# Input projection and mixers' preparation: the elementwise steps of GpSimd put on VectorE

## The chip, the cores and the metric

One core of a Trainium2 chip runs the whole kernel. The metric is the time of one execution on the device in microseconds (us). Five engines work side by side, each through its own queue in order: TensorE (PE: matmuls; PEld: its weight loads), VectorE (DVE), ScalarE (ACT), GpSimd (POOL) and SyncE (SP), which here only issues DMAs. Engines wait for each other by semaphores.

## The reference, cut to what matters

One layer of a hybrid encoder for 656 tokens (16 meta, 512 prompt, 8 x 16 sample), model width 1024:

```
x += 0.5 * SwiGLU_1(RMSNorm(x))
h  = RMSNorm(x);  c = h @ w_in
y  = concat[MLA(c_A), RG-LRU(c_B), GatedDeltaNet(c_C), RWKV7(c_D)] @ w_out;  x += y
x += 0.5 * SwiGLU_2(RMSNorm(x))
final RMSNorm
```

The change lies in the line `c = h @ w_in` and in what prepares the four mixers from its columns: the attention's queries and keys get a rotation (rope) and a normalization, the others a short convolution or a shift by one token, decays, and normalized keys. All of it is float32.

## The kernel before

A float32 product is made of three fast ones: each operand is split into a high part (rounded to the fast format) and a low part (operand minus high part), and high x high, high x low and low x high are summed in PSUM. The split of a weight is one ACT instruction (`whi`, the high part) and one subtraction (`wlo`, the low part).

The execution has four stages: the first SwiGLU (0 to 466 us), the input projection with the mixers' preparation (466 to 793 us), the mixers' tiles with attention over the cache and the output projection (793 to about 1015 us), and the second SwiGLU. The projection has 24 chunks of 128 columns (`project`, L2116). A chunk loads 512 KB of weights on SP's queue, splits them (`wload`, L406: raw, `whi` and `wlo` have two buffers each), and issues 48 matmuls into two of three PSUM buffers (`mm`); DVE then evacuates the two results, multiplied by the row scale `R`. The first chunk (`scale` given) has its `wlo` on DVE, the other 23 on POOL (L2118).

Between the chunks run the preparations as tasks. `Tasks` (L202) is a planner: a modelled clock (`Clock`, L118) charges every instruction, 1.04 ns an element + 70 for DVE, 1.9 ns + 130 for POOL, and the task of the lowest rank that is ready in the model is written next; the compiler's scheduler then orders each engine's queue by that program order and by what its own model has ready. The projection has the last rank (5) and fills what the others leave. POOL's steps before the change are these:

- `rsqrt` (L345): with `pool` true, two DVE instructions and then ten on POOL; with `pool` false, nine on DVE.
- `rope_rows` (L1640): two products on DVE (out of PSUM), their sum on POOL; for `kpe` and for each of four query heads, in two column halves. ACT then squares the head (`s`) and PE sums the squares (`pick`).
- `shifted` (L1157) and `conv` (L1398): a memset and three small copies before and after which ACT starts the mix (`cv`); `rwkv_decay` (L1208) and `rwkv_keys` (L1231): one difference `Wp` and the products with the last decay of each block (`kh`, `bh`); `lru` (L1591): one product; `mla_in` (L1665): one copy of `kpe` into each key head `kh`; `lora_weights` (L1184): the low part of two small weights.
- In the third stage `gdn_front` (L1508): one product `D` a tile; `rwkv_out`, `gdn_out`: the `rsqrt` of tiles 1 and 5; `mla_sample`: an `rsqrt` of 128 columns.

POOL also makes the triangular inverses (`invert`, L852), the products with the sample masks (`sample_tile`) and some copies for the sample's attention.

Of the kernel before, what the change touches and what calls it, by code (L numbers as in the profile page):

```python
# [228 lines left out]
class Kern:  # L229
# [114 lines left out]

    def rsqrt(self, v, n, pool=True):  # L345

        nc = self.nc
        V = nc.vector
        def tmp(nm):
            if n > 32:  # L350
                return self.t(self.mp, [128, 128], "PN" if nm == "rsr" else "Pn", bufs=2)[:v.shape[0], :n]
            return self.t(self.sp, [128, 32], nm, bufs=2)[:v.shape[0], :n]

        y, q = tmp("rsy"), tmp("rsq")
        V.tensor_scalar(y.bitcast(I32), v.bitcast(I32), 1, None, op0=OP.logical_shift_right)
        V.tensor_scalar(y.bitcast(I32), y.bitcast(I32), -1.0, float(0x5f3759df), op0=OP.mult, op1=OP.add)
        if pool:
            r = tmp("rsr")
            G = nc.gpsimd
            G.tensor_tensor(q, y, y, OP.mult)  # L360
            G.tensor_tensor(q, q, v, OP.mult)
            G.tensor_scalar(q, q, -0.5, 1.5, op0=OP.mult, op1=OP.add)
            G.tensor_tensor(y, y, q, OP.mult)
            G.tensor_tensor(q, y, y, OP.mult)
            G.tensor_tensor(q, q, v, OP.mult)
            G.tensor_scalar(r, q, 0.375, -1.25, op0=OP.mult, op1=OP.add)
            G.tensor_tensor(q, q, r, OP.mult)
            G.tensor_scalar(q, q, 1.875, None, op0=OP.add)
            G.tensor_tensor(v, q, y, OP.mult)
            return  # L370

        V.tensor_tensor(q, y, y, OP.mult)
        V.scalar_tensor_tensor(q, q, -0.1875, v, op0=OP.mult, op1=OP.mult)
        V.scalar_tensor_tensor(y, q, 0.5625, y, op0=OP.add, op1=OP.mult)
        V.tensor_tensor(q, y, y, OP.mult)
        V.scalar_tensor_tensor(q, q, 64.0 / 9, v, op0=OP.mult, op1=OP.mult)
        V.scalar_tensor_tensor(q, q, -10.0 / 3, q, op0=OP.add, op1=OP.mult)
        V.scalar_tensor_tensor(v, q, 5.0, y, op0=OP.add, op1=OP.mult)
# [26 lines left out]

    def wload(self, src, kk, dma, eng=None):  # L406
        nc = self.nc
        raw = self.t(self.wp, [128, self.wk, 128], "wraw")
        hi = self.t(self.wp, [128, self.wk, 128], "whi", F32R)
        lo = self.t(self.wp, [128, self.wk, 128], "wlo", F32R)  # L410
        raw, hi, lo = raw[:, :kk], hi[:, :kk], lo[:, :kk]
        dma.dma_start(raw, src)
        nc.scalar.activation(hi, raw, AF.Copy)
        (eng or nc.vector).tensor_tensor(lo, raw, hi.bitcast(F32), OP.subtract)
        return [(hi[:, k], lo[:, k]) for k in range(kk)]
# [32 lines left out]

    def norm_rows(self, acc, blks, pool, inverse=False):

        ps = self.t(self.pp, [128, 512], "mx")[:, :6].rearrange("p (b o) -> p b o", o=1)
        for b in blks:
            c, n = BLK[b]
            self.nc.tensor.matmul(ps[:n, b, :], acc[:, c:c + n], self.one[:, 0:1], start=True, stop=True)
        r = self.compact(ps, 1, blks, 1.0 / 1024, EPS, "nrow")
        ri = self.t(self.sp, [128, 6, 1], "nrowi", bufs=1) if inverse else None
        if inverse:
            self.nc.vector.tensor_copy(ri[:, blks[0]:blks[-1] + 1], r[:, blks[0]:blks[-1] + 1])
        self.rsqrt(r[:, blks[0]:blks[-1] + 1, 0], len(blks), pool)
        if inverse:  # L460
            q = ri[:, blks[0]:blks[-1] + 1]
            self.nc.vector.tensor_tensor(q, q, r[:, blks[0]:blks[-1] + 1], OP.mult)
            return r, ri
        return r
# [9 lines left out]

    def row_scale(self, acc, blks, cols, pool, inverse=False):


        r = self.norm_rows(acc, blks, pool, inverse)
        yield
# [587 lines left out]

    def rows(self, ps, blks, mul, add, tag, pool=True):

# [3 lines left out]
        for i, (_, n, _) in enumerate(blks):  # L1073
            if n < 128:
                V.memset(c[:, i], 1.0)
            V.tensor_scalar(c[:n, i], ps[:n, i], mul, add, op0=OP.mult, op1=OP.add)
        self.rsqrt(c.rearrange("p b c -> p (b c)"), 4 * nb, pool)
        return c
# [58 lines left out]
    def unit(self, sq, mul, dst, l, op):  # L1137
# [5 lines left out]
        r = self.compact(ps, 2, list(range(6)), mul, EPS * mul, "c2")  # L1143
        self.rsqrt(r.rearrange("p b c -> p (b c)"), 12, False)
        e = self.t(self.rp, [128, 6, 2, 64], "exp6", bufs=1)
# [11 lines left out]
    def shifted(self, j, R, sh, tails, x):  # L1157

        nc = self.nc
        V, S, G = nc.vector, nc.scalar, nc.gpsimd  # L1160
        rv = R[:, 529:].rearrange("p (b c) -> p b c", b=8)
        G.memset(R[:, 0:1], 0.0)
        G.tensor_copy(rv[:, :, 0], sh[:, j])
        G.tensor_copy(tails[:, j, 0:1], R[:, 528:529])
        G.tensor_copy(tails[:, j, 1:], rv[:, :, 16])
        t = self.t(self.rp, [128, LC], "cv", bufs=2)
# [17 lines left out]
    def lora_weights(self, src):  # L1184
# [8 lines left out]
        for i in range(2):  # L1193
            r = slice(64 * i, 64 * i + 64)
            nc.gpsimd.tensor_tensor(lo[r], raw[r, i], hi[r, i].bitcast(F32), OP.subtract)
        return hi, lo
# [11 lines left out]
    def rwkv_decay(self, x, wab, rm, dec):  # L1208
# [9 lines left out]
        for hp in range(2):  # L1218
            V.tensor_scalar(Wp[:, hp], Wp[:, hp], 1.0, None, op0=OP.add)
            V.tensor_tensor_scan(Wi[:, hp], rm, Wp[:, hp], 0.0, op0=OP.mult, op1=OP.add)  # L1220
            nc.gpsimd.tensor_tensor(Wp[:, hp], Wi[:, hp], Wp[:, hp], OP.subtract)
            S.activation(W[:, hp], Wi[:, hp], AF.Exp, scale=C1)
# [8 lines left out]
    def rwkv_keys(self, hp, xk, dw, put):  # L1231

        nc = self.nc
        V, S, G = nc.vector, nc.scalar, nc.gpsimd
        W, Wi, Wp, ta = (t[:, hp] for t in dw)
# [22 lines left out]
        for src, n in ((ki, "kh"), (bt, "bh")):  # L1258
            d = rt()
            for a, t, e in ((0, 16, 16), (16, 64, 528), (528, 16, NT)):  # L1260
                v = lambda z: z[:, a:e].rearrange("p (c t) -> p c t", t=t)
                G.tensor_tensor(v(d), v(src), v(W)[:, :, t - 1:t].to_broadcast([128, (e - a) // t, t]), OP.mult)
            put(n, hp, d)
# [112 lines left out]
    def rwkv_out(self, cx, oT, y):  # L1376
# [10 lines left out]
        yield  # L1387
        es = self.spread(self.rows(self.sums(sq, bl), bl, 1.0 / 64, GN_EPS, "c4", cx["b"] not in (2, 3, 4)), bl)
        yield
# [8 lines left out]
    def conv(self, c, buf, j, tails, w, bias=None):  # L1398

        V, G = self.nc.vector, self.nc.gpsimd  # L1400
        cv = c[:, 531:].rearrange("p (b t) -> p b t", b=8)
        G.memset(c[:, 0:3], 0.0)
        G.tensor_copy(cv[:, :, 0:3], buf[:, j])
        G.tensor_copy(tails[:, j, 0], c[:, 528:531])
        G.tensor_copy(tails[:, j, 1:], cv[:, :, 16:19])
        y = self.t(self.rp, [128, LC], "cv", bufs=2)
# [101 lines left out]
    def gdn_front(self, ti, X, scr, gt, ctxs):  # L1508
# [14 lines left out]
        for c0, T, b in blks:  # L1523
# [12 lines left out]
            S.activation(D, D, AF.Exp)  # L1536
            G.tensor_tensor(D, D, be[:T, b].unsqueeze(2).to_broadcast([T, 4, T]), OP.mult)
            yield
# [31 lines left out]
    def gdn_out(self, cx, oT, y):  # L1570
# [5 lines left out]
        yield  # L1576
        es = self.spread(self.rows(self.sums(sq, bl), bl, 1.0 / 64, EPS, "c4", cx["b"] not in (2, 3, 4)), bl)
        yield
# [12 lines left out]
    def lru(self, j, xc, gb, w, h0, hl):  # L1591
# [21 lines left out]
        V.scalar_tensor_tensor(b, a, 1.0, b, op0=OP.add, op1=OP.mult)  # L1613
        nc.gpsimd.tensor_tensor(b, b, ti, OP.mult)

# [24 lines left out]
    def rope_rows(self, dst, ps, c0, n):  # L1640
# [4 lines left out]
        V.tensor_tensor(a[64:96, :n], ps[96:128, :n], self.rope[96:128, c0:c0 + n], OP.mult)  # L1645
        self.nc.gpsimd.tensor_tensor(dst[64:96, c0:c0 + n], dst[64:96, c0:c0 + n], a[64:96, :n], OP.add)

# [17 lines left out]
    def mla_in(self, cq, ckv, sm, w, outs):  # L1665
# [38 lines left out]
        for h in range(4):  # L1704
# [13 lines left out]
            for c0, n in ((0, 400), (400, 128)):  # L1718
                ps = self.t(self.pp, [128, 512], "mx")
                T_.matmul(ps[:64, :n], wuk[:, h], cn[:, c0:c0 + n], start=True, stop=True)  # L1720
                S.activation(k[:64, c0:c0 + n], ps[:64, :n], AF.Copy)
            G.tensor_copy(k[64:96], kpe[64:96, :528])
            s = self.t(self.mp, [128, NT], "s3", bufs=1)
# [13 lines left out]
        V.tensor_scalar(qr, qr, 1.0 / 96, EPS, op0=OP.mult, op1=OP.add)  # L1737
        self.rsqrt(qr.rearrange("p b c -> p (b c)"), 24, False)
        V.tensor_tensor(qr, qr, rr[:, 0].unsqueeze(2).to_broadcast([128, 6, 4]), OP.mult)
# [95 lines left out]
    def mla_sample(self, new, w, caches, y):  # L1835
# [63 lines left out]
        self.rsqrt(ss[:, :128], 128)  # L1899
        self.rsqrt(ss[:, 128:], 4, False)  # L1900
        yield
# [101 lines left out]
def build(tc, A, O):  # L2003
    with ExitStack() as ctx:
# [18 lines left out]
        with ExitStack() as f:  # L2023
# [38 lines left out]
            def scale():  # L2062
                yield from K.row_scale(acc0, allb, cols, False, True)
                K.acc = K.t(K.hp_, [128, NT], "acc")
# [25 lines left out]
        with ExitStack() as f:  # L2090
# [25 lines left out]
            def project(c, ev, scale=None):  # L2116
                with tc.high_priority() if scale else ExitStack():
                    w = K.wload(A["w_in"][c], 8, nc.sync, None if scale else G)  # L2118
                ps = [K.t(K.pp, [128, 512], "mm", bufs=3) for _ in range(2)]
# [73 lines left out]
            def gate_chunks():  # L2193
                s_ = K.row_scale(K.acc, allb, cols, False)
                yield from plain(7, sm, s_)
# [301 lines left out]
        with ExitStack() as f:  # L2497
# [13 lines left out]
            def last(h):  # L2511
                r = K.norm_rows(K.acc, [b for b in fb if (b > 3) == h], False)
                yield
# [10 lines left out]

            K.ffn(x, fcols, lambda: K.row_scale(acc, fb, fcols, False, True), F, "norm_ffn2", norm=last, rows=False)
        pctx.close()
# [118 lines left out]
```

## Time and profile before

| | us |
|---|---|
| median of three runs | 1526.97 (1524.2 to 1529.06) |
| the profiled execution | 1526.97 |
| its span | 1525.0 |
| PE, DVE, ACT, POOL busy | 1448.5, 1094.0, 610.1, 195.4 |
| mean granted TensorE clock | 0.969 |

The span is what the trace covers; some 2 us lie around it. A busy PE is not PE at its peak, since the ends of matmuls are modelled, so that what it waits for is read from its waits. The granted clock has two levels here: 1.00 is 2.4 GHz and 0.50 is 1.2 GHz; a value between them for a stretch is a mixture.

### The profile page before, as it was taken

What the parts mean: (1) busy time and instruction counts of PE and PEld (TensorE: products, weight loads), DVE (VectorE), ACT (ScalarE), POOL (GpSimd) and SP (SyncE); (2) the same over time, 40 slices, a digit from 0 to 9 for tenths busy, and PEclk for the clock granted to TensorE, in tenths of its full rate; (3) what the DMA queues carried; (4) which work ended last, traced back from release to release, by engine and by line L of the source; (5) the groups of instructions that cost most, each with busy time, mean ns of one, the idle gap of its engine ahead of it and who ended that gap; (6) DMA issues with size and microseconds to landing.
All of it is one profiled execution on the core that took longest, in us unless ns stands there. A gap on an engine that the chain in (4) does not pass through costs nothing.

```text
span 1525.0 us, 26202 instructions
## 1 busy us (share of the span) xinstructions
PE 1448.5 (95%) x10158; PEld 1349.1 (88%) x10158; DVE 1094.0 (72%) x2408; ACT 610.1 (40%) x1162; POOL 195.4 (13%) x392
## 2 busy tenths in 40 slices
PE   7999999999999989999987999999999999999996
PEld 6899999999998757878776877689999999999996
DVE  7987858686885367664765555685996966878787
ACT  6534525252442253354423323232652533434351
POOL 0000000000003333122532523510000000000000
PEclk9999999999999999999888989999999999999997
DMA  8131222223224201212267443384122222222221
GB/s 274 46 107 56 81 75 69 95 70 98 70 85 151 64 32 37 86 55 97 100 208 192 114 111 93 93 242 151 56 80 73 90 91 84 87 81 84 81 58 69
DMA packets 106636, 148.14 MB, mean 97 GB/s; under 512 B 20160, under 2 KB 68304, under 8 KB 106512
## 3 DMA queue, kind: packets, MB, share of 16 engines
q1 hardware_dynamic: 103376, 143.99, 30.1%
q10 hardware_dynamic: 3136, 2.47, 0.6%
q8 instruction: 80, 1.31, 0.4%
q14 instruction: 44, 0.36, 0.1%
HBM read 119.88 MB, written 26.56 MB: 96 GB/s over the span
## 4 chain that ended last, share of the span: by engine, by line
PE 79%; DVE 9%; issue 3%; POOL 3%; ACT 3%; DMA 2%; SPq 0%; ACTq 0%; DVEq 0%; POOLq 0%
PE mx L189 63%; PE mm L189 17%; DVE x L189 2%; DVE rsq L189 1%; DVE n L189 1%; POOL qh L189 1%; DVE P L189 1%; POOL kx L189 1%; DMA r<-in_w_out 0%; DVE acc L189 0%; POOL rsq L189 0%; DMA lrow<-q 0%; DVE rx L189 0%; DVE row L189 0%; DMA scr_rw<-kx 0%
## 5 line engine op out<-in xcount | busy, mean ns | idle before, releaser
L189 ACT ACTIVATE whi<-wraw 128x512 fp32r<-128x512 f32 (+2 forms) x260 | 168.0, 649 | 262.2 <-PE mx L189 164.4
L189 PE MATMUL mx<-f,whi 128*128 128x256 f32 (+4 forms) x1200 | 258.9, 309 | 0.0
L189 PE MATMUL mm<-n,whi 128*128 128x400 f32 (+2 forms) x1024 | 213.1, 327 | 11.7 <-ACT n L189 6.4
L189 PEld LDWEIGHTS mx<-f,whi 128*128 128x128 f32 x1200 | 192.5, 189 | 0.5 <-ACT f L189 0.2
L189 PE MATMUL mx<-n,whi 128*128 128x320 f32 (+1 forms) x1088 | 188.3, 312 | 2.7 <-ACT n L189 2.4
L189 DVE TENSOR_TENSOR wlo<-wraw,whi 128x512 fp32r<-128x512 f32 (+2 forms) x233 | 155.8, 670 | 40.5 <-ACT whi L189 38.1
L189 PEld LDWEIGHTS mm<-n,whi 128*128 128x128 f32 x1024 | 164.4, 195 | 21.5 <-ACT n L189 6.4
L189 PEld LDWEIGHTS mx<-n,whi 128*128 128x128 f32 x1088 | 167.7, 189 | 3.8 <-ACT n L189 2.8
L189 ACT ACTIVATE whi<-wsum 128x512 fp32r<-128x512 f32 x160 | 100.5, 631 | 176.1 <-PE mx L189 140.6
L189 PE MATMUL mx<-e,whi 128*128 128x320 f32 (+1 forms) x904 | 159.3, 312 | 0.0
L189 PE MATMUL mx<-f,wlo 128*128 128x384 f32 (+4 forms) x600 | 150.8, 309 | 0.0
L189 PEld LDWEIGHTS mx<-e,whi 128*128 128x128 f32 x904 | 140.8, 189 | 0.3 <-DVE mx L189 0.2
L189 DVE TENSOR_TENSOR wlo<-wsum,whi 128x512 fp32r<-128x512 f32 x160 | 109.9, 688 | 35.1 <-ACT whi L189 35.1
L189 PE MATMUL mm<-n,wlo 128*128 128x256 f32 (+2 forms) x512 | 122.5, 320 | 0.0
L189 PE MATMUL mx<-n,wlo 128*128 128x320 f32 (+1 forms) x544 | 106.1, 311 | 0.0
L189 PEld LDWEIGHTS mx<-f,wlo 128*128 128x128 f32 x600 | 98.7, 189 | 0.0
L189 PE MATMUL mx<-e,wlo 128*128 128x320 f32 (+1 forms) x452 | 91.3, 311 | 0.0
L189 DVE SCALAR_TENSOR_TENSOR x<-mx,x 128x256 f32<-128x256 f32 (+2 forms) x130 | 61.1, 484 | 38.3 <-PE mx L189 37.8
L189 PEld LDWEIGHTS mx<-n,wlo 128*128 128x128 f32 x544 | 87.0, 189 | 0.2 <-DVE wlo L189 0.2
L189 PEld LDWEIGHTS mm<-n,wlo 128*128 128x128 f32 x512 | 83.8, 192 | 2.7 <-issue 2.6
L189 PE MATMUL mm<-f,whi 128*128 128x400 f32 (+2 forms) x272 | 83.2, 322 | 0.0
L189 PEld LDWEIGHTS mx<-e,wlo 128*128 128x128 f32 x452 | 73.0, 189 | 0.1
(590 smaller groups left out, 2503.7 us busy)
## 6 DMA issues: line engine op xcount, KB each, us to landing
wraw<-in_f2w SPq DMA_DIRECT2D x22, 1024.0 KB, 5.1
wraw<-in_f1w SPq DMA_DIRECT2D x21, 1024.0 KB, 5.1
wraw<-in_w_in SPq DMA_DIRECT2D x24, 512.0 KB, 3.7
wraw<-in_f1w SPq DMA_DIRECT2D x12, 512.0 KB, 3.7
wraw<-in_f2w SPq DMA_DIRECT2D x12, 512.0 KB, 3.7
scr_rw<-kx SPq DMA_DIRECT2D x16, 328.0 KB, 2.3
wraw<-in_f1w SPq DMA_DIRECT2D x8, 640.0 KB, 4.0
wraw<-in_f2w SPq DMA_DIRECT2D x8, 640.0 KB, 4.0
```

The source lines that it names most:

```text
L189: return f(*a, **k)
```

## The change

Each elementwise step of POOL named in the list above goes to DVE; `rsqrt` has only its form of nine DVE instructions left (`eng` and `pool` are gone). The inverses, the sample masks and the copies for the sample's attention (`cs`, `es`, `qe`, `QE`, `Pn`) stay on POOL. The planner's costs are as they were, so that it now charges these steps to DVE and may write tasks in another order.

```diff
-    def rsqrt(self, v, n, pool=True):
+    def rsqrt(self, v, n):
...
-        if pool:
-            r = tmp("rsr")
-            G = nc.gpsimd
-            G.tensor_tensor(q, y, y, OP.mult)
...
-            G.tensor_tensor(v, q, y, OP.mult)
-            return
...
-        (eng or nc.vector).tensor_tensor(lo, raw, hi.bitcast(F32), OP.subtract)
+        nc.vector.tensor_tensor(lo, raw, hi.bitcast(F32), OP.subtract)
...
-        G.memset(R[:, 0:1], 0.0)
-        G.tensor_copy(rv[:, :, 0], sh[:, j])
-        G.tensor_copy(tails[:, j, 0:1], R[:, 528:529])
-        G.tensor_copy(tails[:, j, 1:], rv[:, :, 16])
+        V.memset(R[:, 0:1], 0.0)
+        V.tensor_copy(rv[:, :, 0], sh[:, j])
+        V.tensor_copy(tails[:, j, 0:1], R[:, 528:529])
+        V.tensor_copy(tails[:, j, 1:], rv[:, :, 16])
...
-            nc.gpsimd.tensor_tensor(lo[r], raw[r, i], hi[r, i].bitcast(F32), OP.subtract)
+            nc.vector.tensor_tensor(lo[r], raw[r, i], hi[r, i].bitcast(F32), OP.subtract)
...
-            nc.gpsimd.tensor_tensor(Wp[:, hp], Wi[:, hp], Wp[:, hp], OP.subtract)
+            nc.vector.tensor_tensor(Wp[:, hp], Wi[:, hp], Wp[:, hp], OP.subtract)
...
-                G.tensor_tensor(v(d), v(src), v(W)[:, :, t - 1:t].to_broadcast([128, (e - a) // t, t]), OP.mult)
+                V.tensor_tensor(v(d), v(src), v(W)[:, :, t - 1:t].to_broadcast([128, (e - a) // t, t]), OP.mult)
...
-        G.memset(c[:, 0:3], 0.0)
-        G.tensor_copy(cv[:, :, 0:3], buf[:, j])
+        V.memset(c[:, 0:3], 0.0)
+        V.tensor_copy(cv[:, :, 0:3], buf[:, j])
...
-            G.tensor_tensor(D, D, be[:T, b].unsqueeze(2).to_broadcast([T, 4, T]), OP.mult)
+            V.tensor_tensor(D, D, be[:T, b].unsqueeze(2).to_broadcast([T, 4, T]), OP.mult)
...
-        nc.gpsimd.tensor_tensor(b, b, ti, OP.mult)
+        nc.vector.tensor_tensor(b, b, ti, OP.mult)
...
-        self.nc.gpsimd.tensor_tensor(dst[64:96, c0:c0 + n], dst[64:96, c0:c0 + n], a[64:96, :n], OP.add)
+        self.nc.vector.tensor_tensor(dst[64:96, c0:c0 + n], dst[64:96, c0:c0 + n], a[64:96, :n], OP.add)
...
-            G.tensor_copy(k[64:96], kpe[64:96, :528])
+            V.tensor_copy(k[64:96], kpe[64:96, :528])
...
-                    w = K.wload(A["w_in"][c], 8, nc.sync, None if scale else G)
+                    w = K.wload(A["w_in"][c], 8, nc.sync)
```

## Rows read from the trace of the kernel before

**Rows 1.** Stages: us; PE, PEld, DVE, ACT, POOL busy (instructions); clock, DMA share, GB/s.

```profile
466.00:793.00 327.00, 299.74 (x1775) 248.31 (x1775) 194.58 (x466) 125.41 (x228) 113.54 (x148) 0.94 0.27 86
793.00:1000.00 207.00, 194.11 (x1973) 155.42 (x1975) 121.29 (x349) 64.37 (x158) 76.35 (x219) 0.94 0.48 133
```

**Rows 2.** What PE waited for from 466 to 793 us: sum, times, longest.

```profile
PE mx L189 <- ACT s L189: 6.1, 4, 2.2
PE mx L189 <- DVE P L189: 5.3, 4, 2.7
PE mx L189 <- ACT exp L189: 4.6, 4, 2.1
PE mm L189 <- DVE raw L189: 2.2, 1, 2.2
PE mx L189 <- DVE mqr L189: 1.8, 1, 1.8
PE mx L189 <- DVE kx L189: 1.6, 2, 1.2
PE mx L189 <- POOL mr L189: 1.5, 1, 1.5
PE mx L189 <- POOL mkr L189: 0.9, 1, 0.9
```

**Rows 3.** Instructions in order of time, POOL and DVE: start, us, what.

```profile
592.26 2.39 POOL L189 TENSOR_TENSOR wlo<-wraw,whi 128x1024 fp32r<-128x1024 f32 x1 [1.60 <-ACT whi L189]
592.35 2.33 DVE L189 SCALAR_TENSOR_TENSOR rsq<-rsq 128x12 f32<-128x12 f32 x1
...
680.62 2.34 POOL L189 TENSOR_TENSOR wlo<-wraw,whi 128x1024 fp32r<-128x1024 f32 x1 [2.65 <-ACT whi L189]
680.70 2.51 DVE L189 TENSOR_SCALAR P<-P,ars 128x400 f32<-128x400 f32 x1
```

**Rows 4.** DVE and POOL groups of one shape, 466 to 793 us: busy, mean ns.

```profile
L189 DVE TENSOR_SCALAR P<-P,ars 128x528 f32<-128x528 f32 x4 | 2.0, 492 | 0.1
L189 DVE TENSOR_TENSOR wlo<-wraw,whi 128x1024 fp32r<-128x1024 f32 x1 | 1.2, 1204 | 0.0
L189 DVE TENSOR_TENSOR kt<-kt,rx 128x656 f32<-128x656 f32 x2 | 1.6, 825 | 0.0
L189 DVE TENSOR_TENSOR cq<-mm,R 128x400 f32<-128x400 f32 x2 | 1.1, 575 | 6.6 <-PE mm L189 6.6
L189 DVE COPY hl<-lr 128x8 f32<-128x8 f32 x2 | 0.3, 162 | 0.0
...
L189 POOL TENSOR_TENSOR wlo<-wraw,whi 128x1024 fp32r<-128x1024 f32 x23 | 55.7, 2420 | 92.5 <-ACT whi L189 56.6 <-PE mx L189 11.9 <-ACT y_mla L189 10.6
```

**Rows 5.** An rsqrt's first and last step: on POOL (ten steps), on DVE (last seven).

```profile
577.72 0.22 POOL L189 TENSOR_TENSOR rsq<-rsy 128x20 f32<-128x20 f32 x1 [0.91 <-DVE rsy L189]
...
582.62 0.23 POOL L189 TENSOR_TENSOR mkr<-rsq,rsy 128x20 f32<-128x20 f32 x1
...
751.99 0.17 DVE L189 TENSOR_TENSOR rsq<-rsy 128x12 f32<-128x12 f32 x1
...
753.22 0.17 DVE L189 SCALAR_TENSOR_TENSOR c<-rsq,rsy 128x12 f32<-128x12 f32 x1
```

**Rows 6.** ACT's split of a chunk's weights, two chunks following, in order of time.

```profile
491.50 1.06 ACT L189 ACTIVATE whi<-wraw 128x1024 fp32r<-128x1024 f32 x1 [5.44 <-PE mm L189]
498.76 1.06 ACT L189 ACTIVATE whi<-wraw 128x1024 fp32r<-128x1024 f32 x1 [6.20 <-PE mm L189]
```

**Rows 7.** Granted clock by stretch: the columns of rows 1.

```profile
580.00:590.00 10.00, 7.76 (x38) 6.54 (x39) 4.74 (x15) 0.77 (x1) 2.64 (x8) 0.67 0.00 0
630.00:640.00 10.00, 8.52 (x46) 6.86 (x46) 6.44 (x17) 3.43 (x10) 3.35 (x3) 0.73 0.25 68
728.00:742.00 14.00, 13.52 (x33) 8.11 (x34) 11.25 (x15) 9.39 (x18) 6.39 (x8) 0.63 0.11 37
```

**Rows 8.** Second SwiGLU's low parts on DVE, 793 us to the end.

```profile
L189 DVE TENSOR_TENSOR wlo<-wraw,whi 128x512 fp32r<-128x512 f32 x108 | 74.1, 686 | 21.4 <-ACT whi L189 20.6
```

More of the change, by code (lines that the diff above doesn't have):

```diff
@@ L350, in tmp @@
             if n > 32:
-                return self.t(self.mp, [128, 128], "PN" if nm == "rsr" else "Pn", bufs=2)[:v.shape[0], :n]
+                return self.t(self.mp, [128, 128], "Pn", bufs=2)[:v.shape[0], :n]
             return self.t(self.sp, [128, 32], nm, bufs=2)[:v.shape[0], :n]
@@ L356, in rsqrt @@
         V.tensor_scalar(y.bitcast(I32), y.bitcast(I32), -1.0, float(0x5f3759df), op0=OP.mult, op1=OP.add)
-        if pool:
-            r = tmp("rsr")
-            G = nc.gpsimd
-            G.tensor_tensor(q, y, y, OP.mult)
[L361 to L368, printed above, removed]
-            G.tensor_tensor(v, q, y, OP.mult)
-            return
         V.tensor_tensor(q, y, y, OP.mult)
@@ L403, in wide, with wload @@
         return self.t(self.pp, [128, 512], "mx")
-    def wload(self, src, kk, dma, eng=None):
+    def wload(self, src, kk, dma):
         nc = self.nc
@@ L447, in sumsq, with norm_rows @@
             nc.vector.tensor_tensor(acc[:, a:e], acc[:, a:e], s, OP.add)
-    def norm_rows(self, acc, blks, pool, inverse=False):
+    def norm_rows(self, acc, blks, inverse=False):
         ps = self.t(self.pp, [128, 512], "mx")[:, :6].rearrange("p (b o) -> p b o", o=1)
@@ L458, in norm_rows @@
             self.nc.vector.tensor_copy(ri[:, blks[0]:blks[-1] + 1], r[:, blks[0]:blks[-1] + 1])
-        self.rsqrt(r[:, blks[0]:blks[-1] + 1, 0], len(blks), pool)
+        self.rsqrt(r[:, blks[0]:blks[-1] + 1, 0], len(blks))
         if inverse:
@@ L473, in along, with row_scale @@
         return pt
-    def row_scale(self, acc, blks, cols, pool, inverse=False):
-        r = self.norm_rows(acc, blks, pool, inverse)
+    def row_scale(self, acc, blks, cols, inverse=False):
+        r = self.norm_rows(acc, blks, inverse)
         yield
@@ L1066, in sums, with rows @@
         return ps
-    def rows(self, ps, blks, mul, add, tag, pool=True):
+    def rows(self, ps, blks, mul, add, tag):
         V = self.nc.vector
@@ L1076, in rows @@
             V.tensor_scalar(c[:n, i], ps[:n, i], mul, add, op0=OP.mult, op1=OP.add)
-        self.rsqrt(c.rearrange("p b c -> p (b c)"), 4 * nb, pool)
+        self.rsqrt(c.rearrange("p b c -> p (b c)"), 4 * nb)
         return c
@@ L1143, in unit @@
         r = self.compact(ps, 2, list(range(6)), mul, EPS * mul, "c2")
-        self.rsqrt(r.rearrange("p b c -> p (b c)"), 12, False)
+        self.rsqrt(r.rearrange("p b c -> p (b c)"), 12)
         e = self.t(self.rp, [128, 6, 2, 64], "exp6", bufs=1)
@@ L1159, in shifted @@
         nc = self.nc
-        V, S, G = nc.vector, nc.scalar, nc.gpsimd
+        V, S = nc.vector, nc.scalar
         rv = R[:, 529:].rearrange("p (b c) -> p b c", b=8)
-        G.memset(R[:, 0:1], 0.0)
-        G.tensor_copy(rv[:, :, 0], sh[:, j])
-        G.tensor_copy(tails[:, j, 0:1], R[:, 528:529])
-        G.tensor_copy(tails[:, j, 1:], rv[:, :, 16])
+        V.memset(R[:, 0:1], 0.0)
+        V.tensor_copy(rv[:, :, 0], sh[:, j])
+        V.tensor_copy(tails[:, j, 0:1], R[:, 528:529])
+        V.tensor_copy(tails[:, j, 1:], rv[:, :, 16])
         t = self.t(self.rp, [128, LC], "cv", bufs=2)
@@ L1233, in rwkv_keys @@
         nc = self.nc
-        V, S, G = nc.vector, nc.scalar, nc.gpsimd
+        V, S = nc.vector, nc.scalar
         W, Wi, Wp, ta = (t[:, hp] for t in dw)
@@ L1387, in rwkv_out @@
         yield
-        es = self.spread(self.rows(self.sums(sq, bl), bl, 1.0 / 64, GN_EPS, "c4", cx["b"] not in (2, 3, 4)), bl)
+        es = self.spread(self.rows(self.sums(sq, bl), bl, 1.0 / 64, GN_EPS, "c4"), bl)
         yield
@@ L1398, in conv @@
     def conv(self, c, buf, j, tails, w, bias=None):
-        V, G = self.nc.vector, self.nc.gpsimd
+        V = self.nc.vector
         cv = c[:, 531:].rearrange("p (b t) -> p b t", b=8)
-        G.memset(c[:, 0:3], 0.0)
-        G.tensor_copy(cv[:, :, 0:3], buf[:, j])
-        G.tensor_copy(tails[:, j, 0], c[:, 528:531])
-        G.tensor_copy(tails[:, j, 1:], cv[:, :, 16:19])
+        V.memset(c[:, 0:3], 0.0)
+        V.tensor_copy(cv[:, :, 0:3], buf[:, j])
+        V.tensor_copy(tails[:, j, 0], c[:, 528:531])
+        V.tensor_copy(tails[:, j, 1:], cv[:, :, 16:19])
         y = self.t(self.rp, [128, LC], "cv", bufs=2)
@@ L1576, in gdn_out @@
         yield
-        es = self.spread(self.rows(self.sums(sq, bl), bl, 1.0 / 64, EPS, "c4", cx["b"] not in (2, 3, 4)), bl)
+        es = self.spread(self.rows(self.sums(sq, bl), bl, 1.0 / 64, EPS, "c4"), bl)
         yield
@@ L1737, in mla_in @@
         V.tensor_scalar(qr, qr, 1.0 / 96, EPS, op0=OP.mult, op1=OP.add)
-        self.rsqrt(qr.rearrange("p b c -> p (b c)"), 24, False)
+        self.rsqrt(qr.rearrange("p b c -> p (b c)"), 24)
         V.tensor_tensor(qr, qr, rr[:, 0].unsqueeze(2).to_broadcast([128, 6, 4]), OP.mult)
@@ L1899, in mla_sample @@
         self.rsqrt(ss[:, :128], 128)
-        self.rsqrt(ss[:, 128:], 4, False)
+        self.rsqrt(ss[:, 128:], 4)
         yield
@@ L2062, in scale @@
             def scale():
-                yield from K.row_scale(acc0, allb, cols, False, True)
+                yield from K.row_scale(acc0, allb, cols, True)
                 K.acc = K.t(K.hp_, [128, NT], "acc")
@@ L2193, in gate_chunks @@
             def gate_chunks():
-                s_ = K.row_scale(K.acc, allb, cols, False)
+                s_ = K.row_scale(K.acc, allb, cols)
                 yield from plain(7, sm, s_)
@@ L2511, in last @@
             def last(h):
-                r = K.norm_rows(K.acc, [b for b in fb if (b > 3) == h], False)
+                r = K.norm_rows(K.acc, [b for b in fb if (b > 3) == h])
                 yield
@@ L2523, in last @@
                                                                          x[:, k - 1:k + 1, a:a + n])
-            K.ffn(x, fcols, lambda: K.row_scale(acc, fb, fcols, False, True), F, "norm_ffn2", norm=last, rows=False)
+            K.ffn(x, fcols, lambda: K.row_scale(acc, fb, fcols, True), F, "norm_ffn2", norm=last, rows=False)
         pctx.close()
```

## The prediction

> **What bounds the kernel now.** I read the busy times of the stages first. From 466 to 793 us PE is busy 299.7 of 327 us, DVE 194.6, ACT 125.4 and POOL 113.5; POOL's other large share, 76.4 us, lies behind 793 and is mostly work that stays there [rows 1]. No engine but PE is near full, so the stage is bound by PE together with the places where PE stands still, 27.3 us, and by the stretches in which its clock is halved. The waits of PE say what it stood still for: 24.0 us in eight entries [rows 2]. Only 2.4 us name POOL (`mr`, `mkr`). The rest names DVE (`P`, `raw`, `mqr`, `kx`: 10.9 us) and ACT (`s`, `exp`: 10.7 us), so the third view is what DVE did at those times. The reader is to see pairs: a `wlo` of POOL begins, some 0.1 us later a DVE instruction begins that should be short, and it ends when POOL's ends. A step of an rsqrt over 12 columns took 2.33 us, where its likes take 0.17 [rows 3, 5]; the scaling of `P` over 400 columns took 2.51, where 528 columns take 0.49 [rows 3, 4]. Twelve DVE instructions of this stage take over 2 us in this way. All have two inputs from SBUF or are a scaling within SBUF; evacuations out of PSUM run on undisturbed beside them. The waits of PE for `P`, `mqr` and `exp` hang on these.
>
> The Trainium skill (SBUF — State Buffer, "Who interferes with whom") says the same as a rule: DVE and GpSimd share one pair of SBUF ports, whoever comes first holds it for its whole instruction, and a DVE instruction with two SBUF inputs or in a two-port mode is blocked; the trace agrees, with 2.33 us under a `wlo` of 2.39.
>
> **The low parts.** 23 `wlo` of 2.42 us leave POOL and come to DVE at 1.20, the price of the one that is there already [rows 4]: 27.7 us. Does PE come to wait for weights? ACT splits a chunk's weights at the time an earlier chunk ends, one chunk each 7.26 us (491.50 to 498.76), in 1.06 us [rows 6]; POOL's `wlo` is then done 3.5 us after that, DVE's would be some 2.3 us after, and the chunk is needed only when the next is through. So nothing on PE's path is lost by place. What it can lose is order: the `wlo` now stands in DVE's queue behind a wait for ACT, and evacuations, softmax and rsqrt steps stand behind it. The nearest rows: in the second SwiGLU 108 such `wlo` on DVE cost 21.4 us of idle, 0.2 us each [rows 8]; POOL stood 56.6 us for ACT's `whi` in front of these 23, 2.5 us each [rows 4]. So 4.6 to 56.6 us of DVE's time; I take the lower end, since it is the row of the same engine and step with the order made by the same scheduler.
>
> **The sums, products and copies.** With prices by columns [rows 4]: rope, ten sums at no more than 0.575, 5.8 us; two `Wp` and two `lr` at 0.825, 3.3; four `kh`/`bh` products in three pieces, 0.825 + 2 x 0.16, 4.6; four copies of `kpe` at 0.49, 2.0; two small low parts at 0.575, 1.2; 64 memsets and small copies of `conv` and `shifted` at 0.16, 10.2. Together 27.1 us. No DMA moves queue; the stores `scr_rw` of `kh` and `bh` are still on SP and only come earlier.
>
> **The rsqrts.** `mkr` goes through ten POOL steps from 577.72 to 582.85, 5.1 us; seven DVE steps take 1.4 us (751.99 to 753.39) [rows 5]. `mr` and `mkr` thus add 2.8 us to DVE. Past 793 us the four of tiles 1 and 5, the one of 128 columns and five products `D` follow; the stage's clock and PE share (194.1 of 207) show little to win [rows 1], and I take 0, with 2 us either way.
>
> **DVE's balance.** New on DVE: 27.7 + 27.1 + 2.8 + 4.6 (the low end of the waits) = 62 us. Gone: what POOL blocks. The twelve long ones alone give back about 20 us (2.2 us each, less 0.2 to 0.8 for the work itself); the upper end is all of POOL's moved time beside DVE, some 50 us. So DVE goes from 194.6 to between 207 and 237 us of a stage a little over 300: fuller, not full.
>
> **What PE gets back**, entry by entry of its waits [rows 2]. `P`, 5.3: the scaling falls from 2.5 to 0.5, back 4.5. `exp`, 4.6, behind rsqrts that were stopped for 2.3: back 3.5. `mqr`, 1.8: all. `mr` and `mkr`, 2.4: back 2.2. `s`, 6.1, behind the rope sums: the sum now follows its products on the same engine, while POOL overlapped them; where nothing interfered the end stays where it was, where POOL stood under other work it comes earlier: back 4. `raw` and `kx`, 3.8: back 2.5. Sum 18.5 us. Against it stands DVE's larger load of 13 to 42 us, which delays chains without a lock; no row prices what part reaches PE. It could be none; it could be as much as the locks did, 24.0 us of PE for at least 20 us of DVE, which would eat everything. I take a third of the gain, 6 us, since the scheduler sets a `wlo` by its readiness, whereas a lock hits whatever comes second. Left: 12.5 us.
>
> **The clock.** After standing still PE ran at the halved clock for part of three stretches: a granted clock of 0.67 over 10 us, 0.73 over 10, 0.63 over 14, that is 3.3 + 2.7 + 5.2 = 11.2 us of full-speed work missing [rows 7]. They follow the waits for `mqr` and `mkr`, for `P`, and the one before the small matmuls of `rwkv_decay`, in that order. The third has ACT and the scan behind it as well and is likely to stay; of the first two, 6 us, I count 4.5. Bounds: 0 and 11.2.
>
> Sum: 12.5 + 4.5 = 17 us; 1526.97 - 17 = **1510**. The profiled execution is itself the median run (span 1525.0 and 2 around it), so no correction is due.
>
> **The planner** charges the moved steps to DVE and may write tasks in another order. It knows nothing of the locks. The nearest price is one chunk of the projection that comes too early or too late, 7.3 us either way [rows 6]; it stands in the range and not in the sum.
>
> **Rivals.** (A) All comes back: 18.5 + 11.2 = 30, and with what the second and third stage may add (2) and a part of the smaller waits, 35: 1492. For it: no engine is full. Against: DVE's load. (B) The waits only change their name: PE's next late releaser, ACT (`s` and `exp` stand first and third already [rows 2]) or DVE's own queue, eats the gain: 1525, no change. The Trainium skill (Perfetto Trace Analysis, "Optimizing Scalar/DVE Operations") states a rule that would make it so, that moving work between GpSimd and DVE might not help as they share a port; but it is written of relieving a full DVE, and the trace has DVE at 60% with the blocked time on PE's path. By that rule the time is (B)'s. (C) Slower: DVE's queue stands at the head `wlo` until ACT has split the weights, as POOL stood. Place: each chunk's change. If all 56.6 us come with it, and 0.6 of it (DVE's busy share, 194.6 of 327) holds something that PE needs, that is 34 us lost; less the 17 gained, +17: 1544. It decides from 28 us on, 1.2 us a chunk, which is more than ACT's whole split of 1.06 [rows 6], so ACT itself would have to come late; it does so when PE frees the weight buffer late. (D) That POOL's locks do not end: the inverses and masks stay on POOL, but in the stage before 793 only the sample's copies do, 3 to 4 us; no time of its own.
>
> **How the numbers follow.** Forecast 0.60, around 1510, 1499 to 1521; (A) 0.14, 1492; (B) 0.13, 1525; (C) 0.13, 1544, or anywhere above 1532. About 0.3% (4.6 us) is what a measurement of this kernel can tell from no change. Faster: the forecast, (A), and a little of (B): 0.76. Same: 0.12. Slower: 0.12. The range runs from (A)'s 1492 to 1532, the forecast plus a chunk out of place and another 12 us of the gain eaten by DVE's load (1510 + 7.3 + 12 = 1529), and a little over; it leaves out (C) and the far side of (A), 0.17.
>
> **What would show it.** Right: the stage to the end of the last chunk is some 17 us shorter; no DVE instruction of 12 to 24 columns takes 2 us there; PE's waits for `P`, `mqr`, `mkr`, `mr` together fall from 9.5 to below 3 us; the clock around 583 and 634 us is not halved; POOL has under 10 us in the stage; the first, third and fourth stages keep their lengths within 3 us. Wrong: DVE idle before `wlo` for ACT's `whi` over 28 us and waits of PE for `raw` or `whi`/`wlo` over 10 us would mean (C); the same sum of PE's waits under other names means (B). A third stage that changes by 5 us or more means that the planner's order counts for more than I gave it.

## The result

The changed kernel takes 1510.93 us (median of 4 runs, 1505.42 to 1511.54), the kernel before beside it 1527.71 (1524.2 to 1529.06): a ratio of 0.9886, 95% interval 0.9857 to 0.9915. The forecast of 1510 is met. Its parts are not: the projection stage won twice what was forecast, and more than half of that was lost behind it.

The profiled execution of the changed kernel has a span of 1509.2 us and a mean granted clock of 0.966 (before: 1525.0 and 0.969). Its page, busy time of each engine and the chain that ended last:

```profile
PE 1448.6 (96%) x10158; PEld 1354.1 (90%) x10158; DVE 1108.6 (73%) x2582; ACT 608.9 (40%) x1162; POOL 68.5 (5%) x197
PE 88%; DVE 6%; DMA 2%; ACT 2%; issue 1%; POOL 1%; SPq 0%; ACTq 0%; DVEq 0%
```

PE's share of that chain is 88% (79% before), POOL's 1% (3% before), and DVE's busy time has grown by 14.6 us only. For the stages, four marks of PE are read from the timelines: the end of the last matmul on the projection's weights, the first matmul of the third stage, the first of the second SwiGLU (which here closes the third stage; before, it comes at 1073.4 us, not at the about 1015 named above), and the end.

| us | projection ends | third stage starts | second SwiGLU starts | end |
|---|---|---|---|---|
| before | 785.0 | 787.1 | 1073.4 | 1525.0 |
| after | 750.1 | 765.4 | 1057.9 | 1509.2 |
| difference | -34.9 | -21.7 | -15.5 | -15.8 |

The stages cut at these marks, of before (first fence) and after (second), in the columns of [rows 1]:

```profile
466.00:785.00 319.00, 294.92 (x1744) 245.28 (x1745) 189.41 (x451) 123.27 (x219) 113.54 (x148) 0.94 0.25 81
787.00:1073.00 286.00, 262.94 (x2489) 220.89 (x2487) 175.60 (x501) 92.57 (x226) 81.60 (x239) 0.95 0.51 148
```

```profile
466.00:750.00 284.00, 282.55 (x1744) 239.60 (x1744) 190.67 (x572) 123.00 (x219) 3.73 (x10) 0.97 0.26 81
750.00:770.00 20.00, 9.22 (x33) 5.32 (x32) 10.27 (x20) 2.34 (x5) 0.00 (x0) 0.61 0.95 294
765.00:1058.00 293.00, 271.71 (x2488) 228.77 (x2488) 181.40 (x539) 91.15 (x226) 64.55 (x183) 0.91 0.49 140
```

The same 1744 matmuls take 284 us in place of 319, with PE standing 1.5 us in place of 24.1. DVE does 121 instructions more in the same busy time (190.7 against 189.4). What PE waited for from 466 to 770 us (as [rows 2]):

```profile
PE mx L189 <- DMA xin<-scr_rw: 5.6, 1, 5.6
PE mx L189 <- DVE kx L189: 4.9, 1, 4.9
PE mm L189 <- DVE wlo L189: 0.6, 1, 0.6
PE mx L189 <- PE mm L189: 0.2, 1, 0.2
PE mm L189 <- DVE raw L189: 0.2, 1, 0.2
```

Up to the last chunk the eight entries of [rows 2] are gone but for a rest of `raw`. The two long ones are new in size, and both lie behind the last chunk, between 750 and 765 us; the `kx` here is one of `rwkv_keys`, whereas 1.2 of the 1.6 us of [rows 2] stood before `rwkv_decay`, at 728 us. DVE's groups from 466 to 750 us (as [rows 4]):

```profile
L189 DVE TENSOR_TENSOR wlo<-wraw,whi 128x1024 fp32r<-128x1024 f32 x24 | 29.2, 1218 | 0.3 <-ACT exp L189 0.2
L189 DVE TENSOR_SCALAR P<-P,ars 128x400 f32<-128x400 f32 x4 | 1.7, 424 | 0.0
L189 DVE SCALAR_TENSOR_TENSOR rsq<-rsq 128x12 f32<-128x12 f32 x7 | 1.2, 167 | 0.1
L189 DVE COPY rtail<-raw 128x8 f32<-128x8 f32 x8 | 1.3, 161 | 0.0
```

No DVE instruction from 466 us to the projection's end lasts over 1.55 us (17 did before, 12 of them over 2.0). The scaling of `P` that took 2.51 us takes 0.42, the rsqrt step that took 2.33 takes 0.17 [rows 3]. DVE stood 0.3 us before its 24 `wlo`.

How much of DVE's busy time was lock can be read by matching its instructions of the two stages by tile and shape. The 447 of before whose shape also stands in the stage after took 35.6 us more than at the mean of after: 27.4 us of it in those that ran beside a `wlo`, 8.1 beside other work of POOL, and 0.1 in the 283 that ran beside none.

The clock of the two stretches that were to recover, the third of [rows 7] at its new place, and the join of the stages:

```profile
580.00:590.00 10.00, 10.00 (x70) 9.02 (x69) 8.73 (x31) 2.35 (x3) 0.50 (x2) 1.00 0.26 87
630.00:640.00 10.00, 9.93 (x65) 8.48 (x64) 6.42 (x23) 3.98 (x7) 0.00 (x0) 1.00 0.14 40
716.00:730.00 14.00, 14.00 (x81) 12.16 (x81) 11.98 (x31) 9.93 (x18) 0.00 (x0) 0.88 0.40 126
754.00:775.00 21.00, 12.84 (x66) 7.96 (x66) 10.30 (x29) 3.98 (x14) 0.74 (x2) 0.51 0.92 280
```

### The profile page after: what moved, and what is told of

The parts are those of the page before. It is cut to its first block, busy times and chain, and to the rows that moved or that the text cites. A ratio compares the mean times of both kernels' runs of the same rounds, so it can differ in the third digit from the quotient of the medians.

```text
span 1509.2 us, 26132 instructions
## 1 busy us (share of the span) xinstructions
PE 1448.6 (96%) x10158; PEld 1354.1 (90%) x10158; DVE 1108.6 (73%) x2582; ACT 608.9 (40%) x1162; POOL 68.5 (5%) x197
## 4 chain that ended last, share of the span: by engine, by line
PE 88%; DVE 6%; DMA 2%; ACT 2%; issue 1%; POOL 1%; SPq 0%; ACTq 0%; DVEq 0%
PE mx L189 67%; PE mm L189 21%; DVE x L189 2%; DMA r<-in_w_out 1%; DVE n L189 1%; DVE kx L189 1%; DVE acc L189 1%; DMA xin<-scr_rw 0%; DVE row L189 0%; DVE wlo L189 0%; ACT whi L189 0%; ACT row L189 0%; DMA x<-in_x 0%; SPq L189 0%; POOL Pb L189 0%
## 5 line engine op out<-in xcount | busy, mean ns | idle before, releaser
L189 DVE TENSOR_TENSOR wlo<-wraw,whi 128x512 fp32r<-128x512 f32 (+2 forms) x256 | 183.6, 718 | 41.4 <-ACT whi L189 38.8
```

What stands on the lines that cost most here:

```text
L189: return f(*a, **k)
```

## The experiments

Three readings stand against each other. Locks: POOL's `wlo` holds up DVE, DVE holds up PE. Order: the planner charges the moved steps to DVE and writes other tasks first, and that is what moved the time. Load: DVE is fuller, and that costs. All runs together; "clock" is span x (1 - granted clock), the full-speed time that halved stretches take away if PE has work all through them, as a mean over the n executions of that kernel, and "rest" is the span less that; the marks are those of the profiled execution.

| kernel | median us (n) | ratio, 95% | clock | rest | projection ends | third stage starts | second SwiGLU starts |
|---|---|---|---|---|---|---|---|
| before | 1527 to 1530 (36) | | 48 | 1478 | 785.0 | 787.1 | 1073.4 |
| after | 1510.9 (4) | 0.9886 [0.9857, 0.9915] | 47 | 1460 | 750.1 | 765.4 | 1057.9 |
| x1 low parts alone on DVE | 1512.4 (4) | 0.9903 [0.9884, 0.9921] | 42 | 1468 | 765.5 | 776.9 | 1059.3 |
| z1 the same, order of before | 1513.0 (5) | 0.9913 [0.9894, 0.9933] | 42 | 1469 | 765.3 | 778.2 | 1058.9 |
| x2 after, low parts on POOL | 1524.7 (10) | 0.9981 [0.9961, 1.0001] | 47 | 1476 | 773.8 | 780.3 | 1071.1 |
| x3 after, POOL reads | 1546.8 (4) | 1.0130 [1.0100, 1.0159] | 67 | 1478 | 780.9 | 795.5 | 1092.3 |
| x4 after, POOL writes | 1506.6 (5) | 0.9861 [0.9838, 0.9885] | 45 | 1461 | 745.4 | 761.2 | 1061.6 |
| x5 before, charged as DVE | 1554.3 (4) | 1.0156 [1.0122, 1.0189] | 64 | 1488 | 790.9 | 793.0 | 1101.1 |
| x6 after, charged as POOL | 1502.6 (4) | 0.9819 [0.9792, 0.9846] | 40 | 1461 | 749.6 | 765.4 | 1051.5 |
| x7 after, third stage on POOL | 1508.3 (4) | 0.9859 [0.9831, 0.9888] | 48 | 1459 | 749.1 | 764.7 | 1053.7 |
| x8 after, rwkv earlier | 1509.1 (4) | 0.9871 [0.9829, 0.9913] | 48 | 1460 | 743.7 | 759.3 | 1052.1 |
| y1 after, gdn first | 1509.1 (4) | 0.9867 [0.9833, 0.9902] | 50 | 1458 | 749.0 | 758.7 | 1054.0 |
| y2 after, own buffer | 1511.0 (4) | 0.9874 [0.9830, 0.9918] | 50 | 1458 | 755.2 | 757.3 | 1061.8 |
| y3 x6 with y1 and y2 | 1518.0 (5) | 0.9931 [0.9906, 0.9956] | 56 | 1461 | 753.8 | 756.0 | 1059.7 |

**x1, the 23 low parts alone.**

```diff
-                    w = K.wload(A["w_in"][c], 8, nc.sync, None if scale else G)
+                    w = K.wload(A["w_in"][c], 8, nc.sync)
```

> The kernel before with one edit: the 23 low parts of the projection's weights go from POOL to DVE, everything else stays on POOL. Locks: nearly all of what POOL read in SBUF in this stage is taken away, so the DVE instructions of over 2 us between 466 us and the end of the projection are gone or down to one or two, PE's waits for P, exp and mqr fall by over 8 us together, and the whole time is 1508 to 1518 us, near to the changed kernel's 1511. Order: if the changed kernel's gain came from the order that the planner wrote after all the other moves, this kernel has about half of it or none, 1518 to 1530. DVE's load: 27.7 us more on DVE, and if that counts, above 1528.

1512.4 us: this one edit has nearly the whole gain of the kernel, with 19.5 of the 34.9 us of the stage. What PE waits for from 466 to 800 us, the first entries:

```profile
PE mx L189 <- DVE kx L189: 5.0, 2, 3.0
PE mx L189 <- ACT s L189: 4.9, 4, 1.7
PE mx L189 <- DMA xin<-scr_rw: 2.6, 1, 2.6
PE mm L189 <- DVE raw L189: 2.0, 1, 2.0
PE mx L189 <- POOL mr L189: 1.6, 1, 1.6
PE mx L189 <- DVE rp L189: 1.4, 1, 1.4
PE mx L189 <- POOL mkr L189: 0.7, 1, 0.7
PE mx L189 <- DVE P L189: 0.4, 1, 0.4
```

`P` fell from 5.3 to 0.4, `exp` (4.6) and `mqr` (1.8) are gone [rows 2]: these were locks. `s` (4.9 of 6.1), `mr` and `mkr` (2.3 of 2.4) stay: they hang on the rope sums and rsqrts that this kernel leaves on POOL.

**x2, the same edit undone in the changed kernel.**

```diff
-                    w = K.wload(A["w_in"][c], 8, nc.sync)
+                    w = K.wload(A["w_in"][c], 8, nc.sync, None if scale else G)
```

> The changed kernel with one edit: the 23 low parts of the projection's weights are back on POOL, the rope sums, rsqrts, copies and decays stay on DVE. Locks: some 10 or more DVE instructions of over 2 us come back in the projection's stage, PE's waits there go from 12 us up to over 20 us, and the time is 1518 to 1528 us. Order or the small moves: the time stays at 1508 to 1515 us, since only 23 instructions have gone to an engine that stands idle.

The gain is gone: 1524.7 us, which can't be told from before. 17 DVE instructions of over 2 us are back, and PE stands 18.1 us up to the projection's end (over 20 were expected). Two pairs, POOL's `wlo` and what stands under it on DVE:

```profile
581.17 2.57 POOL L189 TENSOR_TENSOR wlo<-wraw,whi 128x1024 fp32r<-128x1024 f32 x1 [4.09 <-ACT whi L189]
581.38 2.38 DVE L189 SCALAR_TENSOR_TENSOR rsy<-rsq,rsy 128x12 f32<-128x12 f32 x1
...
702.57 2.36 POOL L189 TENSOR_TENSOR wlo<-wraw,whi 128x1024 fp32r<-128x1024 f32 x1 [11.03 <-ACT whi L189]
702.59 2.38 DVE L189 COPY rtail<-raw 128x1 f32<-128x1 f32 x2
```

So the other moves are worth 11 us in the stage (773.8 against 785.0) and nothing in the whole while the low parts stay on POOL. On top of x1 they are worth 15 us in the stage (750.1 against 765.5), and in the whole again nothing that these runs show (1510.9 against 1512.4).

**x3 and x4, work added to the idle POOL.** The result of the added work is not used; DVE, PE and ACT keep the changed kernel's program order.

```diff
         nc.vector.tensor_tensor(lo, raw, hi.bitcast(F32), OP.subtract)
+        if pool:
+            f, g = (t.rearrange("p k m -> p (k m)")[:, :NT] for t in (raw, hi.bitcast(F32)))
+            for _ in range(2):
+                nc.gpsimd.eng.tensor_tensor(self.acc, f, g, OP.subtract)
```

> The changed kernel, with work added on the idle POOL: at each of the 23 weight chunks two subtractions over 656 columns that read the chunk's raw and high parts and write a buffer that nobody uses; 46 instructions of about 1.55 us, 71 us of POOL in all. The order of the instructions on DVE, PE and ACT is the changed kernel's. Locks: DVE instructions with two inputs in SBUF that begin under one of these last as long as the rest of it, some 1 to 1.5 us more; 15 to 30 of them; the stage loses 8 to 17 us and the whole kernel 5 to 17 (1516 to 1528 us). Order: nothing of DVE's work is touched, so 1511 us within 3.

In x4 the last two lines are five memsets of the same buffer.

> The control for the added reads: the changed kernel, with five memsets over 656 columns on POOL at each of the 23 weight chunks instead, which read nothing and write the same unused buffer. POOL is busy for about as long. If what blocks DVE is that POOL reads in SBUF with two inputs, the time is the changed kernel's 1511 us within 3, and no DVE instruction of under 25 columns lasts over 1 us. If any work on POOL blocks DVE, it loses as much as the kernel with the added reads does, 5 to 17 us.

The reads cost 36 us (1546.8), twice the upper end of what was expected, 30.8 of it up to the projection's end (8 to 17 expected); the writes cost nothing that these runs show (1506.6, from 1504.1 to 1515.1). In x3, 21 DVE instructions of the stage last over 1.55 us, the new `wlo` among them:

```profile
756.84 4.09 POOL L404 TENSOR_TENSOR acc<-wraw,whi 128x656 f32<-128x656 f32 x2 [3.12 <-issue]
756.88 2.61 DVE L189 TENSOR_TENSOR wlo<-wraw,whi 128x1024 fp32r<-128x1024 f32 x1
```

The table says where 36 us come from: the rest is 18 us up, in keeping with the locks, and the clock term 20. Of x4, DVE's groups from 466 to 560 us, where the memsets lie (75.8 of 94 us of POOL):

```profile
L189 DVE TENSOR_TENSOR wlo<-wraw,whi 128x1024 fp32r<-128x1024 f32 x9 | 11.0, 1218 | 0.1
L189 DVE TENSOR_SCALAR rsy<-rsy 128x12 int32<-128x12 int32 x1 | 0.7, 672 | 0.0
L189 DVE TENSOR_TENSOR rsq<-rsy 128x12 f32<-128x12 f32 x2 | 0.3, 170 | 0.1
```

Instructions with two inputs run at their own price under a memset; a scaling doesn't (0.67 us, 0.17 without) but waits for one memset of 0.65 us at most. So x4 is a control for two things at once, reading and length. For the two-input instructions it is the reading that counts; for scalings both may, and the runs don't separate them. Order alone explains neither x2 nor x3.

**x5 and x6, the planner's charge.** The engine of each moved step stays, the model charges the other one.

```diff
+        self.gx = Engine(self.nc.clk, tc.nc.gpsimd, "v")
...
-                    w = K.wload(A["w_in"][c], 8, nc.sync, None if scale else G)
+                    w = K.wload(A["w_in"][c], 8, nc.sync, None if scale else K.gx)
```

and so for every moved step; x6 has `tc.nc.vector` charged as `"g"` in the changed kernel.

> The kernel before, every step on the engine where it was (POOL), but the planner that writes the order of the tasks charges the moved steps to DVE, as it does in the changed kernel. Locks: the DVE instructions of over 2 us stay (8 to 18 of them up to the end of the projection's matmuls), that end stays at 775 to 795 us, the whole at 1520 to 1535. Order: if the planner's different order was the gain, the projection ends near the changed kernel's 750 us and the whole is 1508 to 1515.

> The changed kernel, every moved step on DVE, but the planner charges these steps to POOL, as it does in the kernel before. Locks: no DVE instruction of over 2 us before the projection's end, which stays at 745 to 765 us; the whole 1504 to 1518, what differs is only how the stage behind it is joined on. Order: 1520 or more.

The order that comes with the change is a loss in itself: 1554.3 us with the old engines, which neither expectation of x5 had, and without it the changed kernel takes 1502.6 in place of 1510.9, the lowest median of all. The projection ends where the engines say (791 and 750 us, and 12 DVE instructions of over 2 us stand in x5 as before); the order acts in the third stage. For x6 the gain lies in the clock term (40 in place of 47), while the rest is the changed kernel's (1461 and 1460). Its windows in x5, x6 and, for later, y2:

```profile
793.00:1101.00 308.00, 272.65 (x2488) 228.40 (x2487) 175.19 (x502) 92.95 (x227) 80.52 (x239) 0.91 0.48 138
```

```profile
765.00:1052.00 287.00, 266.69 (x2491) 221.41 (x2492) 178.58 (x540) 91.87 (x227) 63.70 (x183) 0.94 0.50 143
```

```profile
757.00:1062.00 305.00, 280.61 (x2490) 233.34 (x2489) 181.33 (x543) 91.71 (x227) 63.41 (x183) 0.89 0.49 142
```

In x5 PE stands 35 us of 308 (23 of 286 before), 8.7 of it at once for POOL's rsqrt of 128 columns:

```profile
PE mx L189 <- POOL ss L189: 8.7, 1, 8.7
```

In x6 against after, PE's standing is the same (20 and 21 us); the granted clock is 0.94 in place of 0.91.

**x7, the third stage's steps back on POOL** (the products `D`, the rsqrts of tiles 1 and 5 and of 128 columns, each call as in the kernel before):

```diff
-            V.tensor_tensor(D, D, be[:T, b].unsqueeze(2).to_broadcast([T, 4, T]), OP.mult)
+            G.tensor_tensor(D, D, be[:T, b].unsqueeze(2).to_broadcast([T, 4, T]), OP.mult)
```

> The changed kernel, with the steps of the third stage that moved back on POOL: the products D, the rsqrts of tiles 1 and 5 and the one of 128 columns. The prediction gave these 0 within 2 us. If so, 1509 to 1513. If they are what makes the stage from the projection's end to the second SwiGLU longer than before (278 us against 258), this kernel gets back a good part of the 18 us that are lost there: 1495 to 1505. If POOL's reads lock DVE there as well, it loses: 1513 to 1520.

1508.3 (1507.4 to 1511.2) against 1505.4 to 1511.5: no difference that these runs show. So these moves are not what took back the 18 us that the expectation speaks of. The third stage of x7's profiled execution, its fastest, is 3.5 us shorter than the changed kernel's; a cost of that size cannot be excluded.

**x8, y1 and y2, the join of the stages.** Three ways at the 15.3 us between the last chunk and the third stage. x8: `tasks.add(0.4, rwkv(...))` in place of 2. y1: `for k in (1, 0)` in place of `range(2)` where the first fronts are added. y2:

```diff
-        kk = rt()
+        kk = self.t(self.rp, [128, NT], "gsq", bufs=2)
```

> The changed kernel with one number changed: the planner's rank of the task that prepares rwkv goes from 2 to 0.4, so that it asks for its keys earlier. In the changed kernel PE stands 10.5 us between 750 and 765 us, for kx of DVE and for the transfer of scr_rw, and the clock is halved for 20.5 us behind it. If the keys' chain on DVE is what comes late there, the stall shrinks by 5 to 10 us and the halved stretch is shorter: 1498 to 1506. If the stall only moves to another task (conv, the latents), 1509 to 1513; if the earlier chain pushes the softmax behind it, up to 1518.

> The changed kernel with the two first steps of the third stage exchanged: gdn's front comes before rwkv's, so that PE's queue does not begin the stage with the matmul that waits for rwkv's rows. If the 15 us between the projection's last matmul and the stage's first (of which 10.5 us is PE's standing still) is only that the wrong step stands at the head of PE's queue, gdn's matmuls fill about 5 of them, the clock is halved for less long, and the time is 1500 to 1507 us. If gdn's rows or its chain are as late, or DVE's backlog holds both, 1508 to 1514.

> The changed kernel, where the squares of rwkv's keys get a buffer of their own instead of one of the five kx buffers, so that the keys of the second head pair need not wait until the first pair's kx are stored. If the reuse of kx is what makes the keys' chain the last thing of the projection stage (ACT's square of the second pair stands 4.5 us for DVE's kx), the chain ends 4 to 10 us earlier, PE's wait for kx of 4.9 us goes away, and the time is 1500 to 1507 us. If DVE's queue is what holds them (DVE is busy nearly all of 742 to 757 us), 1508 to 1513.

x8 moved the projection's end, 6.4 us earlier, and not the join. y1 shortened the join to 9.7 us. y2 closed it, 2.1 us as before, so the shared `kx` buffers were indeed why the keys came last; the projection ended 5.1 us later for it. None made the whole faster (1509.1, 1509.1, 1511.0). In y2 the third stage begins 8 us earlier and lasts 12 us longer, at a granted clock of 0.89. The stall at the join is real, and taking it away is worth nothing that these runs show. That is no sharp bound: y2's four executions lie between 1502.9 and 1515.7 us, and the profiled one is the slowest of them.

**y3, x6 with y1 and y2.**

> The three together: every moved step on DVE, the planner charging them to POOL as in the kernel before, gdn's front first and a buffer of its own for the keys' squares. If they add up: the 1503 us of the order of before, less what the other two give (0 to 12 us): 1492 to 1503. If the planner's new arrangement spoils it, up to 1510.

1518.0: they don't add up, and neither expectation had it. The rest is that of x6, 1461 us, the clock term 56 in place of 40.

**z1, the low parts alone with the order of before** (x1, with the low parts charged to POOL):

```diff
-                    w = K.wload(A["w_in"][c], 8, nc.sync, None if scale else G)
+                    w = K.wload(A["w_in"][c], 8, nc.sync, None if scale else K.gx)
```

> The kernel before with the 23 low parts of the projection's weights on DVE and nothing else: the planner goes on charging them to POOL, so its order of tasks is that of the kernel before, and the third stage is untouched. Locks alone: the projection's last matmul comes at 755 to 770 us (785 before), at most three DVE instructions of over 1.5 us are left there, and the whole is 1503 to 1513 us, as good as the changed kernel or better, since the planner's order, which cost 8 us or more where it could be compared, stays. If the other moves carried half of the gain, or the order of before costs with these low parts, 1514 to 1524.

1513.0, as x1 (1512.4). For this edit alone the charge makes no difference, so the order's cost must come from charging the other steps. The third stages of x1 and z1 (first and second line), in the columns of [rows 1]:

```profile
777.00:1059.00 282.00, 262.50 (x2487) 220.99 (x2487) 173.98 (x498) 92.32 (x226) 81.74 (x239) 0.95 0.52 147
778.00:1059.00 281.00, 259.86 (x2488) 218.49 (x2488) 174.43 (x499) 92.73 (x227) 81.35 (x239) 0.95 0.52 147
```

By the marks of the table the projection is 20 us shorter in both than before, the join has grown to 11.4 and 12.9 us, and the third stage is not longer than before but shorter: 282.4 and 280.7 us against 286.3, at a granted clock of 0.95 as before.

## Why the prediction was right or wrong

**The mechanism was right.** POOL's `wlo` locks DVE, DVE's lateness stops PE. Taking the `wlo` away brings the time down by 1%, putting them back loses it, and adding reads on POOL to a kernel of unchanged program order loses more than it. The rule of the Trainium skill (SBUF — State Buffer, "Who interferes with whom") holds in each: under a POOL instruction that reads, a 12-column step takes 2.38 us; under one that only writes, a step with two inputs takes its own 0.17.

**What PE gets back in the stage was 22.6, not 12.5.** Entry by entry the prediction gave back 18.5 of 24.0 us and then took a third off for DVE's load. Up to the last chunk PE's standing fell from 24.1 to 1.5 us. The third was the wrong step: DVE's load was put at 13 to 42 us more, and its busy time grew by 1.3, or by 9.3 with the join counted (191.3 up to 787.1 us before, 200.6 up to 765.4 after). The freed time lies within the prediction's 20 to 50 us (some 35 by shapes). What was too high is the new work. The prediction added up 57.6 us of durations; the added instructions take 52 us one by one, but only some 41 us of busy time, since the records of neighbours on DVE overlap. Nor did `wlo` wait for ACT: 0.3 us where 4.6 was taken.

**The clock in the stage gave some 10, not 4.5**: 319 x 0.06 = 19 us missing before, 284 x 0.03 = 9 after. Both stretches counted on went to 1.00, the third rose from 0.63 to 0.88; the upper bound of 11.2 was near.

**So the stage won 34.9 us, not 17**: the 35 that rival A had for the whole kernel, with its mechanism. That no engine was full, the point for it, weighed more than DVE's load, the point against.

**What failed is the passage to the end.** The prediction said of each wait what it returns and not what is late next. It left the third stage at 0 within 2 us and took the projection's gain for the kernel's. Behind the last chunk stands `rwkv_keys` of the second head pair and its stores: join 13.2 us longer, third stage 6.2 longer, together 19.4 of the 34.9 (the second SwiGLU 0.3 shorter). Two errors, 17.9 us in the stage and 19.4 behind it, cancelled; that the 1510 was hit is luck and not the working.

**What takes it back is only partly settled.** In the join PE stands 10.5 us for the keys and their rows. In the third stage the profiled executions miss 293 x 0.09 = 26 us at halved clock, 286 x 0.05 = 14 before. The planner's order has a part in this: x6, with the order of before, takes 8 us less than the changed kernel, their times don't overlap, and its third stage lasts 286.1 us, as before (286.3), in place of 292.5. The prediction had 7.3 either way in its range and named a third stage changed by 5 us or more as the sign that the order counts for more. But the order of before is no sure gain: y3 has it too and takes 1518.0. The join is not from the order, since z1, with that of before, has one of 12.9 us; and closing it gained nothing that the runs show (y1, y2). Nor does a faster projection lengthen the third stage by itself, since behind those of x1 and z1 it is shorter than before. What sets the granted clock of the third stage (0.95 before, in x1 and z1, 0.94 in x6, 0.91 after, 0.89 in y2) stayed open. Within one kernel, from execution to execution, the span moves by 0.59 us for each us of the clock term (57 executions of the twelve kernels of the experiments), which suggests that the term overstates what the clock costs. Over its four executions the changed kernel's term is 47 us, that of before 48: in the whole, the clock gave nothing, where +4.5 was forecast, and the gain is all in the rest (1478 to 1460).

**The rivals.** B: PE's waits did not change their name within the stage, so the caution of the Trainium skill (Perfetto Trace Analysis, "Optimizing Scalar/DVE Operations"), by which a move between the two engines might not help, did not come true there: the stage won 34.9 us. But for the whole B was half right: the next late thing took half. C: refuted by the 0.3 us. Slower than before came about where POOL kept its work and the order changed (x5), which no rival had, and where reads were added on POOL (x3).

**The signs.** Right: no blocked 12- to 24-column instruction, `P`, `mqr`, `mr` and `mkr` at 0 in place of 9.5, the clock at both places, POOL at 3.73 us, the fourth stage (451.3 us against 451.6). Wrong: the stage's length, by a factor of two, and the third stage's.

## What to carry to other kernels

Look in the trace for instructions that take ten times their like, and for what ran on the neighbour engine then: such time is no load, and yet it is counted as busy and not as idle, so that no view of waits shows it on that engine. Here some 35 of 189 us were of this kind, and moving their cause freed them. Then follow the gain past its stage: say what stands last at the next join, and time the whole, since a stage here won 35 us and the kernel 17. Time the largest single move as well: the 23 low parts alone gave the kernel as much as all moves together, as far as these runs can tell. And where a planner writes the order by engine costs, a move changes the order as well; time the two apart: here the engines were worth 27 us in the order of before (1530.0 to 1502.6) and 43 in the new one (1554.3 to 1510.9), while the new order cost 24 us with the old engines and 8 with the new.

## What was unexpected of the hardware

- The lock catches more than steps with two inputs: copies of one to eight columns were held under `wlo` as well (two in 2.38 us in x2; eight columns take 0.16 us in the changed kernel), and so were scalings.
- It works both ways. In x3, 46 reads of 656 columns on POOL took 1931 ns in the mean, the shortest 1565 and the longest 2601. The twelve longest, all of 2445 ns or more, began while a `wlo` of DVE ran; the second of the pair shown above is one of them.
- In x3 clock and stalls came together: 18 us more in the rest and 20 in the clock term (0.966 to 0.955 in the profiled executions). Yet in y2's profiled execution closing a stall gave no clock back (its third stage has 0.89, after 0.91), though that execution is the slowest of four.
